# Both attentions of a two-layer decoder trunk rebuilt for four heads at a time

## The chip, the cores and the metric

The kernel runs on one core of one Trainium2 chip. The metric is device time in microseconds (us) of one execution, as the median of several runs. The names of the engines are those of the profile: PE is TensorE's matrix multiplication, PEld its weight load, DVE is VectorE, ACT is ScalarE, POOL is GpSimd and SP is SyncE, which here only issues DMA transfers.

## What is computed

A decoder trunk of two layers on x of shape (1, 256, 1024) in float32. Each layer is an attention and then an MLP with a squared ReLU. Layer 0's attention (MoBA) has 16 heads of 64; its blocks are as long as the sequence, so that each query sees only its own block and the attention is plain causal softmax. Layer 1's attention has 12 heads in three groups of four, with windows and dilations of (128, 1), (512, 4) and (2048, 16); the results of the groups are weighted by their softmax denominators, so that the three groups of one head slot form one softmax. q and k are rotated first in both.

```python
def apply_rotary(t, cos, sin):
    t1, t2 = jnp.split(t, 2, axis=-1)
    return jnp.concatenate([t1 * c - t2 * s, t2 * c + t1 * s], axis=-1)

def sq_relu_mlp(x, w_in, w_out):                       # 1024 -> 4096 -> 1024
    return jnp.square(jax.nn.relu(x @ w_in)) @ w_out

h = x
for i in range(2):
    mix = (moba_attention, dilated_attention)[i](h, w_qkv, w_o, cos, sin)
    h = layer_norm(4 ** 0.25 * h + mix, ln_mix_g[i], ln_mix_b[i])
    h = layer_norm(4 ** 0.25 * h + sq_relu_mlp(h, mlp_w_in[i], mlp_w_out[i]), ln_mlp_g[i], ln_mlp_b[i])
```

## The kernel before

**Precision.** The products use the fp32r type. Each float32 operand is split into a high part (the rounded copy) and a low part (the rest), and a product is three matmuls: high by high, high by low and low by high. `split` (L321) makes the two parts, the high one on ACT (L323) and the low one on DVE (L328). `mm` (L332) issues every matmul but the transposes (L627).

**Weights.** SP loads each weight tile of 128 x 1024 (512 KB) into one of four `raw` buffers; ACT and DVE split it into `whi` and `wlo`, ten buffers of each (`NSLOT`). The kernel uses some 180 such tiles, each once. The layer's input stands transposed in `xs`: 1024 features on the partitions of eight tiles, 256 tokens in the columns, the high part beside the low part, so that 512 columns are both.

**Projections.** q and k come out transposed (features on the partitions). The first four q/k tiles are multiplied while x and the weights arrive (`Stage`). For the other q/k tiles `mm_wstat` (L454) runs 24 matmuls of 256 columns each. For an MLP input tile `mm_wstat_wide` (L467) runs 8 of 512 columns (the high weight with both parts of x at once) and 8 of 256 (the low weight with the high part); the two halves of the PSUM bank are added when it is read. The values and the first MLP chunk have x as the stationary operand (`mm_xstat`, L480), and so have all output projections (`mm_rows`, L506): one weight row of 128 x 1024 takes 12 matmuls of 512 columns, for two halves m of the tokens, two accumulators of 512 columns each and three terms.

**Attention.** Heads go in pairs. `rotate` (L536) turns one q and one k tile: ACT copies each half of the tile to the other half's partitions, DVE multiplies by cosine and sine and adds, then q is split into `qhi` and `qlo`, and k is split twice with a mask (`hm`) that keeps one head's rows, into `khi` and `klo` for both heads side by side. `score` (L588) is three matmuls on all 128 rows, for one half of the queries and both heads' keys: 512 columns, or 256 where a half of the queries needs only a half of the keys. Masking with the row's extreme is on DVE (`mask_min`), the exponential with its sum on ACT (`exps`), the scaling on DVE. For the value product the probabilities are transposed on PE into a `tp` bank and copied to `pt` on ACT (L635); `weigh` (L638) then runs a pair of matmuls, each on 64 of PE's columns, one for each head. A stretch of such column-split matmuls between full ones is called a visit here; before, each has one pair of heads. `attn_out` splits the result into `ahi` and `alo` for the output projection.

**Layer norm.** `ln_half` (L708) adds the residual to the accumulators of one half of the tokens, and normalizes. Where something follows, four transposes (L627) bring 512 features of the half into a `tp` bank, from which ACT and DVE write `xs`. The last MLP has m = 1's second accumulator cut into two of 256 columns, one of them in a `tp` bank (`new_acc`, L757), for all of its 32 weight rows.

**PSUM.** There are four `acc` and four `tp` banks. q/k and output accumulators use `acc`; scores, transposes, value products and MLP input tiles use `tp`.

**What sets the order.** No engine's order is written by hand. The program describes its operations in the order of the strings `ORDER0` and `ORDER1` (a step `qk` projects and rotates a pair, `v` projects values, `s` is a pair's scores and softmax, `o` its transposes and value product; `x`, `g` and `b` are loads), with an estimated cost for each. `Plan.order` (L139) then works out a due time for every operation, back from PE's order, and fills each engine's queue by earliest start and earliest due time, with the buffers of every tag as a limit (a tag in `LOOSE` may be taken out of turn if a spare buffer is left). `TAIL` says how many of the last weight rows are done accumulator by accumulator and not row by row.

Of the kernel before, what the change touches and what calls it, by code (L numbers as in the profile page):

```python
# [40 lines left out]
STAGE_HOME = (("raw", 4),) * 4 + (("g", 1), ("b", 1)) + (("tok", 2),) * 2  # L41
# [49 lines left out]
class Plan:  # L91
# [47 lines left out]
    def order(self):  # L139
        clock = {e: BEGIN[e] for e in ("PE", "SP")}  # L140
        bus = 0.0
        for o in self.ops:
            t = max([clock.get(o.eng, 0.0)] + [p.end + latency(p, o) for p in o.preds])
            o.end = t + o.cost
            if o.eng in clock:
                clock[o.eng] = o.end
            if o.xfer:
                bus = o.end = landed(t, bus, o.xfer)
            o.due = t - o.ahead if o.eng == "PE" else None
        t = clock["PE"]  # L150
# [20 lines left out]
        def start_of(o):  # L171
# [7 lines left out]
            for tag, bs in need.items():  # L179
                q = self.queue[tag]  # L180
                spare = 0
                if {id(b) for b in q[: len(bs)]} != {id(b) for b in bs}:
                    if tag not in LOOSE:
                        return None
                    spare = 1
# [65 lines left out]
LOOSE = ("tp",)  # L251

# [4 lines left out]
    "bst mx sm mv rstd ta raw whi wlo g b xs0 xs1 tok m1 ahi alo ropet khi klo v sc1 sc0 pt0 pt1 qhi qlo ident"  # L257
# [5 lines left out]
def tile_trunk(  # L263
# [17 lines left out]
    hmask: bass.AP,  # L281
# [55 lines left out]
    def load_w(src, n=1024):  # L337
        w = W()
        w.raw = mk([P, 1024], F32, "raw", 4)
# [82 lines left out]
    idle = mk([P, 512], F32, "ta", 4)  # L422
# [11 lines left out]
    hm = const(hmask, [P, 2], "hm")  # L434
# [19 lines left out]
    def mm_wstat(ps, w):  # L454
        def go_hi(kt):
            for part in range(2):
                mm(ps.t[:, :S], w.hi.t[:, kt * P : (kt + 1) * P], xs[kt // 4].t[:, kt % 4, part, :], kt + part == 0, False)

        def go_lo(kt):
            mm(ps.t[:, :S], w.lo.t[:, kt * P : (kt + 1) * P], xs[kt // 4].t[:, kt % 4, 0, :], False, kt == KT - 1)  # L460

        for kt in range(KT):
            op("PE", 0.24, lambda kt=kt: go_hi(kt), [(w.hi, 0)] + xk(kt, (0, 1)), [ps])
        for kt in range(KT):
            op("PE", 0.12, lambda kt=kt: go_lo(kt), [(w.lo, 0)] + xk(kt, (0, 1)), [ps])

    def mm_wstat_wide(ps, w):  # L467
        def go_hi(kt):
            both = xs[kt // 4].t[:, kt % 4, :, :].rearrange("p h s -> p (h s)")
            mm(ps.t, w.hi.t[:, kt * P : (kt + 1) * P], both, kt == 0, False)  # L470

        def go_lo(kt):
            mm(ps.t[:, S:], w.lo.t[:, kt * P : (kt + 1) * P], xs[kt // 4].t[:, kt % 4, 0, :], False, kt == KT - 1)

        for kt in range(KT):
            op("PE", 0.229, lambda kt=kt: go_hi(kt), [(w.hi, 0)] + xk(kt, (0, 1)), [ps])
        for kt in range(KT):
            op("PE", 0.12, lambda kt=kt: go_lo(kt), [(w.lo, 0)] + xk(kt, (0, 1)), [ps])
# [27 lines left out]
    def mm_rows(pieces, item, m):  # L506
        (ahi, alo, j), w, pos, total = item
        first, last = pos == 0, pos == total - 1
# [27 lines left out]
    def rotate(ps, ropet):  # L536

        a = mk([P, 512], F32, "ta", 4)
        b = mk([P, 512], F32, "ta", 4)

        def cols(t, i):
            return t.t[:, i * S : (i + 1) * S]

        for i in range(2):
            for h in range(2):
                op(
                    "ACT", act(S),
                    lambda i=i, h=h: nc.scalar.activation(  # L548
                        cols(b, i)[64 * h : 64 * h + 64], ps[i].t[64 - 64 * h : 128 - 64 * h, :S], AF.Copy
                    ),  # L550
                    [ps[i]], [(b, (i, h))],
                )
        for i in range(2):
            tt(S, lambda i=i: cols(a, i), lambda i=i: ps[i].t[:, :S], lambda: ropet.t[:, 0, :], ALU.mult,
               [ps[i], ropet], [(a, i)])
        for i in range(2):
            k = [(b, (i, h)) for h in range(2)]
            tt(S, lambda i=i: cols(b, i), lambda i=i: cols(b, i), lambda: ropet.t[:, 1, :], ALU.mult, k + [ropet], k)
            tt(S, lambda i=i: cols(a, i), lambda i=i: cols(a, i), lambda i=i: cols(b, i), ALU.add, k + [(a, i)], [(a, i)],
               ADD_ENG)  # L560
        q = mk([P, S], F32R, "qhi", 2), mk([P, S], F32R, "qlo", 2)
        split(S, lambda: a.t[:, :S], lambda: q[0].t, lambda: q[1].t, [(a, 0)], [q[0]], [q[1]], sbuf=True)
        hi, lo = mk([P, 2, S], F32R, "khi", 2), mk([P, 2, S], F32R, "klo", 2)
        for h in range(2):
            op(
                "ACT", act(S, 1, True),
                lambda h=h: nc.scalar.activation(hi.t[:, h, :], a.t[:, S:], AF.Copy, scale=hm.t[:, h : h + 1]),  # L567
                [(a, 1), hm], [(hi, h)],
            )
# [558 lines left out]
```

## Time and profile before

| | |
|---|---|
| median of 3 runs | 574.01 us (573.71 to 574.57) |
| span of the profiled execution | 572.5 us |
| DVE, ACT and PE busy, 296 to 380 us (layer 1's attention) | 71.68, 54.88 and 82.93 of 84 us |
| DVE and ACT busy, 135 to 157 us (first MLP) | 18.16 and 15.24 of 22 us |
| read from HBM | 104.01 MB, 184 GB/s over the span |

The first stretch up to 10 us fills the pipeline; layer 0's attention follows, to about 110 us, then the first MLP, layer 1's attention and from about 390 us the second MLP. Busy times are shares of the engine's own time; PE's records overlap each other, so its busy time doesn't say how densely it is filled. A weight load (PEld) lies beside the matmul ahead of it.

### The profile page before, as it was taken

Reading aid. Unit: us, or ns where it says so; the run is one execution under the profiler, and the core shown is the slowest. Engines: PE = TensorE matmul, PEld = TensorE weight load, DVE = VectorE, ACT = ScalarE, POOL = GpSimd, SP = SyncE. Lnnn points to the kernel's source line nnn. Section 1 sums busy time; section 2 is a strip of 40 time slices with the busy share of each in tenths; the row PEclk is TensorE's granted clock in tenths of the full one; section 3 lists DMA queues with packets and bytes.
Section 4 is the critical chain, followed back from the end, with each engine's and each line's share of the span. In section 5 each row is a group of like instructions: output and inputs, shape, how many; then the busy total and the mean of one; then the engine's idle time right before and its main releaser. Section 6 shows DMA issues by size and latency. Waiting matters only on the chain.

```text
span 572.5 us, 8665 instructions
## 1 busy us (share of the span) xinstructions
PE 561.6 (98%) x3234; PEld 487.1 (85%) x3234; DVE 422.6 (74%) x771; ACT 320.6 (56%) x557; POOL 8.4 (1%) x13
## 2 busy tenths in 40 slices
PE   8999999999999999999999999999999999999994
PEld 7898888788888888888888997888888888888884
DVE  5899788898775675675678798987975756756644
ACT  6988688547654454455534678745754544544400
POOL 0000000010000000000000000000000000000000
PEclk9999999999999999999999999999999999999999
DMA  8657652627885765555625434444888655655001
GB/s 319 228 185 259 230 174 76 224 76 261 295 295 195 222 210 189 185 189 181 192 76 184 172 111 148 149 145 148 266 286 262 212 186 186 189 183 181 37 1 73
DMA packets 30281, 105.61 MB, mean 184 GB/s; under 512 B 3488, under 2 KB 4256, under 8 KB 30240
## 3 DMA queue, kind: packets, MB, share of 16 engines
q1 hardware_dynamic: 30240, 105.07, 55.4%
q8 instruction: 25, 0.41, 0.3%
q14 instruction: 16, 0.13, 0.1%
HBM read 104.01 MB, written 1.05 MB: 184 GB/s over the span
## 4 chain that ended last, share of the span: by engine, by line
PE 91%; ACT 3%; DMA 2%; DVE 2%; SPq 0%; issue 0%; DVEq 0%
PE acc L332 51%; PE tp L332 37%; PE tp L627 2%; DMA raw<-in_wv_dram 1%; DMA g<-in_xw_dram 1%; DVE wlo L328 1%; ACT whi L323 1%; ACT ta L548 1%; ACT sc L613 1%; DVE tok L533 0%; SPq L319 0%; ACT khi L567 0%; DVE ta L526 0%; DVE sc L603 0%; ACT ta L791 0%
## 5 line engine op out<-in xcount | busy, mean ns | idle before, releaser
L328 DVE TENSOR_TENSOR wlo<-raw,whi 128x1024 fp32r<-128x1024 f32 (+2 forms) x185 | 221.9, 1205 | 86.5 <-ACT whi L323 85.8
L323 ACT ACTIVATE whi<-raw 128x1024 fp32r<-128x1024 f32 (+2 forms) x184 | 191.6, 1048 | 137.2 <-PE tp L332 59.2
L332 PE MATMUL acc<-whi,ahi 128*128 128x512 f32 (+1 forms) x312 | 119.3, 382 | 0.0
L332 PE MATMUL acc<-wlo,ahi 128*128 128x512 f32 (+1 forms) x312 | 117.3, 380 | 0.0
L332 PE MATMUL tp<-xs,whi 128*128 128x512 f32 x448 | 112.0, 392 | 0.0
L332 PE MATMUL acc<-whi,alo 128*128 128x512 f32 (+1 forms) x312 | 100.7, 379 | 0.0
L332 PEld LDWEIGHTS tp<-xs,whi 128*128 128x128 f32 x448 | 81.1, 189 | 14.9
L332 PEld LDWEIGHTS acc<-whi,ahi 128*128 128x128 f32 x312 | 58.7, 188 | 11.0 <-issue 0.5
L332 PEld LDWEIGHTS acc<-wlo,ahi 128*128 128x128 f32 x312 | 58.7, 188 | 10.5
L332 PE MATMUL acc<-xs,whi 128*128 128x256 f32 x448 | 65.8, 289 | 0.3 <-ACT xs L323 0.3
L332 PEld LDWEIGHTS acc<-whi,alo 128*128 128x128 f32 x312 | 57.1, 188 | 10.4
L332 PEld LDWEIGHTS tp<-xs,wlo 128*128 128x128 f32 x448 | 61.1, 190 | 4.3
L332 PE MATMUL tp<-xs,wlo 128*128 128x256 f32 x448 | 62.8, 283 | 0.0
L332 PEld LDWEIGHTS acc<-xs,whi 128*128 128x128 f32 x448 | 59.3, 194 | 3.2 <-issue 1.7
L323 ACT ACTIVATE ahi<-ta 128x256 fp32r<-128x256 f32 x56 | 22.9, 409 | 27.0 <-DVE ta L533 26.7
L332 PE MATMUL acc<-xs,wlo 128*128 128x256 f32 x224 | 36.7, 286 | 0.0
L332 PEld LDWEIGHTS acc<-xs,wlo 128*128 128x128 f32 x224 | 31.4, 194 | 0.3 <-issue 0.3
L526 DVE TENSOR_TENSOR ta<-tp,ta 128x256 f32<-128x256 f32 x56 | 23.5, 419 | 10.0 <-ACT ta L781 10.0
L781 ACT ACTIVATE ta<-tp 128x256 f32<-128x256 f32 x56 | 21.1, 377 | 15.3 <-PE tp L332 15.2
L332 PE MATMUL acc<-whi,xs 128*128 128x512 f32 (+1 forms) x112 | 28.4, 363 | 0.0
L328 DVE TENSOR_TENSOR alo<-ta,ahi 128x256 fp32r<-128x256 f32 x56 | 23.4, 420 | 5.9 <-ACT ahi L323 5.9
L548 ACT ACTIVATE ta<-acc 64x256 f32<-64x256 f32 x56 | 21.2, 379 | 10.7 <-DVE ta L526 9.8
(85 smaller groups left out, 537.9 us busy)
## 6 DMA issues: line engine op xcount, KB each, us to landing
raw<-in_win_dram SPq DMA_DIRECT2D x64, 512.0 KB, 4.2
raw<-in_wout_dram SPq DMA_DIRECT2D x64, 512.0 KB, 4.3
raw<-in_wqk_dram SPq DMA_DIRECT2D x24, 512.0 KB, 4.4
raw<-in_wo_dram SPq DMA_DIRECT2D x14, 512.0 KB, 3.5
raw<-in_wv_dram SPq DMA_DIRECT2D x8, 512.0 KB, 5.7
g<-in_lng_dram SPq DMA_DIRECT2D x4, 512.0 KB, 5.3
b<-in_lnb_dram SPq DMA_DIRECT2D x4, 512.0 KB, 6.7
raw<-in_wv1a_dram SPq DMA_DIRECT2D x4, 512.0 KB, 3.3
```

Source lines behind the costliest of these rows:

```text
L323: op("ACT", act(n, sbuf=sbuf), lambda: nc.scalar.activation(hi(), src(), AF.Copy), r, whi)
L328: lambda: nc.vector.tensor_tensor(lo(), src(), f32(hi()), op=ALU.subtract), list(r) + list(whi), wlo,
L332: nc.tensor.matmul(out_ap, lhsT, rhs, start=start, stop=stop)
L526: op("DVE", dve(n) + extra, lambda: nc.vector.tensor_tensor(out_ap(), a(), b(), op=alu), r, w)
L548: lambda i=i, h=h: nc.scalar.activation(cols(b, i)[64 * h : 64 * h + 64], ps[i].t[64 - 64 * h : 128 - 64 * h, :S], AF.Copy),
L613: lambda: nc.scalar.activation(e(), e(), AF.Exp, bias=bias(), scale=-1.0, accum_out=total()), r, w,
L627: nc.tensor.transpose(ps.t[:, c : c + P], src(), ident.t)
L781: op("ACT", act(S), lambda: nc.scalar.activation(u(), ps.t[:, S:], AF.Copy), [ps], uk)
```

## The change

**Order.** `ORDER0` and `ORDER1` go by quads of four heads: four quads in layer 0, three in layer 1 (where a quad has two of the three groups' pairs, `quads`), and in layer 1 one `o` step for each unit of three pairs. The planner's due times also regard the operations that wait for a PSUM bank to come free; `SPARE` is 2 and not 1; `NSLOT` is 9 and not 10; `raw` has 5 buffers and not 4; `ta` has three of 1024 columns and not four of 512.

**q and k.** `mm_wide` takes the place of `mm_wstat` and `mm_wstat_wide`, for q/k and MLP tiles alike: four tiles at a time, the first four k tiles of each with the high weight, then the last four of each, then the low weights. The host lays the four tiles of a quad out as q first halves, k first halves, q second halves, k second halves of four heads, 32 features of a head below each other. So the rotation needs no exchange of partitions and the scores no head mask; `hm` and its DMA go.

**Scores.** Each matmul has 32 rows, one head's half: two halves, three terms, 256 columns or 128, and each head writes a `tp` bank of its own. Four heads stand next to each other in the order.

**Value products.** A visit has two pairs (layer 0) or three (layer 1); `pt` has four buffers of 512.

**MLP.** Chunks of four tiles by `mm_wide`. In the last MLP `new_acc` cuts nothing; the cut of the last accumulator begins at the last seven weight rows, whose `tp` piece is added by DVE to the residual apart.

```diff
-TAIL = (5, 5, 6, 8)
-NSLOT = 10
+TAIL = (5, 5, 6, 7)
+NSLOT = 9
+ORDER0 = "qk-0 v-0 qk-1 s-0 o-0 qk-2 s-1 x-0 x-1 o-1 qk-3 s-2 g-0 v-1 s-3 o-2 b-0 o-3"
...
-ORDER1 = "v-01 qk-0 qk-1 s-0 qk-2 s-1 qk-3 s-2 gb-0 qk-4 s-3 o-0 o-1 o-2 qk-5 s-4 s-5 v-10 v-11 o-3 o-4 o-5"
+ORDER1 = "qk-0 qk-1 s-0 qk-2 s-1 gb-0 s-2 v-01 v-10 v-11 o-0 o-1"
+AHEAD1 = (14.0, 6.0)
...
+    def mm_wide(pss, ws):
...
+        def go_hi(ps, w, k0):
+            for kt in range(k0, k0 + 4):
+                both = xs[kt // 4].t[:, kt % 4, :, :].rearrange("p h s -> p (h s)")
+                mm(ps.t, w.hi.t[:, kt * P : (kt + 1) * P], both, kt == 0, False)
+
+        def go_lo(ps, w):
+            for kt in range(KT):
+                mm(ps.t[:, S:], w.lo.t[:, kt * P : (kt + 1) * P], xs[kt // 4].t[:, kt % 4, 0, :], False, kt == KT - 1)
...
+        for k0 in (0, 4):
+            for j, (ps, w) in enumerate(zip(pss, ws)):
+                op("PE", 4 * 0.2268, lambda ps=ps, w=w, k0=k0: go_hi(ps, w, k0), [(w.hi, 0)] + x(k0, k0 + 4),
+                   [ps, (mark, (k0, j))])
+        for ps, w in zip(pss, ws):
+            op("PE", 0.965, lambda ps=ps, w=w: go_lo(ps, w), [(w.lo, 0), mark] + x(0, KT), [ps])
...
+    def rotate(pss, ropet, wide=True):
+
+        u, a, b = [mk([P, 4, S], F32, "ta", 3) for _ in range(3)]
+        for i, ps in enumerate(pss):
+            op("ACT", act(S), lambda i=i, ps=ps: nc.scalar.activation(u.t[:, i, :], ps.t[:, S:] if wide else ps.t[:, :S], AF.Copy),
+               [ps], [(u, i)])
+            if wide:
+                tt(S, lambda i=i: u.t[:, i, :], lambda ps=ps: ps.t[:, :S], lambda i=i: u.t[:, i, :], ALU.add,
+                   [ps, (u, i)], [(u, i)])
...
+            for dst, k in ((a, 0), (b, 1)):
+                tt(512, lambda c=c, dst=dst: dst.t[:, c, :], lambda c=c: u.t[:, c, :],
+                   lambda k=k: ropet.t[:, k : k + 1, :].broadcast_to([P, 2, S]), ALU.mult,
+                   [(u, i) for i in keys] + [ropet], [(dst, h)])
...
+            tt(512, lambda c=c: a.t[:, c, :], lambda c=c: a.t[:, c, :], lambda d=d: b.t[:, d, :], ALU.add if h else ALU.subtract,
+               [(a, h), (b, 1 - h)], [(a, h)])
+            split(512, lambda c=c: a.t[:, c, :], lambda h=h: hi.t[:, h, :, :], lambda h=h: lo.t[:, h, :, :],
+                  [(a, h)], [(hi, h)], [(lo, h)], sbuf=True)
...
+    def score(pss, qk, blocks):
...
+            for i in range(max(len(bl) for bl in blocks)):
+                for h in range(2):
+                    for t, (a, b) in enumerate(((hi, hi), (hi, lo), (lo, hi))):
+                        for n, bl in enumerate(blocks):
+                            if i >= len(bl):
+                                continue
+                            qc, kc, off = bl[i]
+                            r = slice(32 * n, 32 * n + 32)
+                            mm(pss[n].t[:, off : off + kc.stop - kc.start], a.t[r, h, 0, qc], b.t[r, h, 1, kc],
+                               h + t == 0, h + t == 3)
...
+            for p in range(2):
+                weigh(o, p * S, v[0], vc + p * P, pts[p], 0, S, 0, True, False)
+                weigh(o, p * S, v[1], vc + p * P, pts[2], p * S, P, P, False, True)
...
+    def pv_dilated(e, v, vcs, ahi, alo, ahead):
...
+            for kb in range(2):
+                weigh(o, 0, v[0][kb], vcs[0], full[kb], 0, S, 0, kb == 0, kb == 1)
+            for m in range(2):
+                weigh(o, S, v[1][m], vcs[1], diag[0], m * S, P, m * P, True, True)
+                weigh(o2, 0, v[2][m], vcs[2], diag[1], m * S, P, m * P, True, True)
...
-    def new_acc(last=False):
-        acc = [[(psum("acc"), n * 512, 512) for n in range(2)] for _ in range(2)]
-        if last:
-            acc[1] = [acc[1][0], (acc[1][1][0], 512, 256), (psum("tp"), 768, 256)]
-        return acc
+    def new_acc():
+        return [[(psum("acc"), n * 512, 512) for n in range(2)] for _ in range(2)]
...
+            if last and m == 1:
+                acc[1] = [acc[1][0], (acc[1][1][0], 512, S), (psum("tp"), 768, S)]
...
+        quads = (((0, 0), (0, 1)), ((0, 2), (1, 0)), ((1, 1), (1, 2)))
```

The change moves instructions on PE in three places. The first is layer 0's first scores, on PE. `tp` are PSUM banks; `acc_338` (before) and `acc_406` (after) are q/k accumulators, the rows on them the last of a projection. `mm` is L332 before and L345 after. Before:

```order
L332 MATMUL acc_338<-wlo_305,xs_2_75 128x512 x2
L332 MATMUL tp_396<-khi_81,qhi_88 128x512
L332 MATMUL tp_396<-klo_82,qhi_88 128x512
L332 MATMUL tp_396<-khi_81,qlo_89 128x512
L332 MATMUL tp_402<-khi_81,qhi_88 128x256
L332 MATMUL tp_402<-klo_82,qhi_88 128x256
L332 MATMUL tp_402<-khi_81,qlo_89 128x256
```

And after, where the first eight of a quad's 48 score matmuls are shown:

```order
L345 MATMUL acc_406<-xs_2_75,wlo_366 128x256 x4
L345 MATMUL tp_488<-rhi_80 128x256
L345 MATMUL tp_490<-rhi_80 128x256
L345 MATMUL tp_492<-rhi_80 128x256
L345 MATMUL tp_494<-rhi_80 128x256
L345 MATMUL tp_488<-rlo_81,rhi_80 128x256
L345 MATMUL tp_490<-rlo_81,rhi_80 128x256
L345 MATMUL tp_492<-rlo_81,rhi_80 128x256
L345 MATMUL tp_494<-rlo_81,rhi_80 128x256
```

Six matmuls for a pair, into two banks, became groups of four that go round four banks, one for each head.

The second place is the head of layer 1 on PE: the last transposes of the layer norm's second half (`tok` into `tp`), behind them the value projection of the first half (`acc` from `xs` and a weight's high part). Before:

```order
L627 MATMUL tp_3139<-ident_90,tok_719 128x128 x4
L627 MATMUL tp_3145<-ident_90,tok_719 128x128 x4
L332 MATMUL acc_3103<-whi_2967,xs_2_75 128x512 x2
L332 MATMUL acc_3103<-whi_2985,xs_2_75 128x512 x2
L332 MATMUL acc_3161<-whi_2900,xs_1_74 128x512
L332 MATMUL acc_3161<-wlo_2922,xs_1_74 128x512
L332 MATMUL acc_3161<-whi_2900,xs_1_74 128x512
```

After:

```order
L631 MATMUL tp_3055<-ident_86,tok_373 128x128 x4
L631 MATMUL tp_3061<-ident_86,tok_373 128x128 x4
L345 MATMUL acc_3019<-whi_2895,xs_2_75 128x512 x2
L345 MATMUL acc_3019<-whi_2916,xs_2_75 128x512 x2
L345 MATMUL acc_3074<-xs_1_74,whi_2984 128x512 x4
L345 MATMUL acc_3083<-xs_1_74,whi_2997 128x512 x4
L345 MATMUL acc_3092<-xs_1_74,whi_3014 128x512 x4
```

The value projection of the second half (`acc_3161`), which stood next, moved far behind; the first wide q/k matmuls stand there now.

The third place is the value products of layer 1's first unit on PE, with `pt` (transposed probabilities) and `v`; `acc_3659` is a q/k tile. Before, a visit for each of the unit's three pairs, here the first two:

```order
L332 MATMUL acc_3659<-xs_1_74,whi_3389 128x256 x2
L332 MATMUL tp_3694<-pt_692_3674,v_3164 64x256 x2
L332 MATMUL tp_3694<-pt_694_3683,v_3212 64x256 x2
L332 MATMUL acc_3659<-xs_2_75,whi_3389 128x256 x2
L332 MATMUL tp_3714<-pt_697_3697,v_3164 64x128 x2
L332 MATMUL tp_3714<-pt_697_3697,v_3212 64x128 x2
```

After, one visit for the three pairs, with `acc_3688` a value projection:

```order
L345 MATMUL acc_3688<-whi_3401,xs_2_75 128x256 x2
L345 MATMUL tp_3759<-pt_3726,v_3079 64x256 x2
L345 MATMUL tp_3759<-pt_3732,v_3677 64x256 x2
L345 MATMUL tp_3759<-pt_3740,v_3079 64x128 x2
L345 MATMUL tp_3766<-pt_3746,v_3079 64x128 x2
L345 MATMUL tp_3759<-pt_3740,v_3677 64x128 x2
L345 MATMUL tp_3766<-pt_3746,v_3677 64x128 x2
L345 MATMUL acc_3688<-whi_3401,xs_2_75 128x256 x2
L631 MATMUL tp_3788<-ident_86,e_3555 128x128
```

Three visits of one pair became one visit of three, and it moved from among q/k tiles to the end of the last value projection; the second unit's transposes follow it.

More of the change, by code (lines that the diff above doesn't have):

```diff
@@ L251 @@
 LOOSE = ("tp",)
+SPARE = 2
 BANKS = ("tp", "acc")
 LAYOUT = (
-    "bst mx sm mv rstd ta raw whi wlo g b xs0 xs1 tok m1 ahi alo ropet khi klo v sc1 sc0 pt0 pt1 qhi qlo ident"
+    "bst mx sm mv rstd ta raw whi wlo g b xs0 xs1 tok m1 ahi alo rhi rlo v e pt ropet ident"
 ).split()
@@ L338, in load_w @@
         w = W()
-        w.raw = mk([P, 1024], F32, "raw", 4)
+        w.raw = mk([P, 1024], F32, "raw", 5)
         w.hi = mk([P, 1024], F32R, "whi", NSLOT)
@@ L504, in mm_xstat, with mm_rows @@
                 )
-    def mm_rows(pieces, item, m):
+    def mm_rows(pieces, item, m, opens=False):
         (ahi, alo, j), w, pos, total = item
-        first, last = pos == 0, pos == total - 1
+        first, last = pos == 0 or opens, pos == total - 1
         t = slice(m * P, (m + 1) * P)
@@ L534, in stt @@
         )
[L536 to L563, printed above, removed]
-        for h in range(2):
[L565 to L569, printed above, removed]
-            stt(
-                S, 1, lambda h=h: lo.t[:, h, :], lambda: a.t[:, S:], lambda h=h: hm.t[:, h : h + 1],
-                lambda h=h: f32(hi.t[:, h, :]), ALU.mult, ALU.subtract, [(a, 1), hm, (hi, h)], [(lo, h)],
-            )
-        return q, (hi, lo)
@@ L583, in tile_trunk @@
+    def proj_qk(ws):
+        pss = [psum("acc") for _ in ws]
+        mm_wide(pss, ws)
+        return pss
     first_ps = [psum("acc") for _ in range(NFIRST)]
@@ new lines, in weigh, with attn_out @@
+    def weigh(o, o0, v, vc, pt, p0, n, c0, start, stop):
+        for h in range(2):
+            c = slice(vc + 64 * h, vc + 64 * h + 64)
+            mm(o.t[64 * h : 64 * h + 64, o0 + c0 : o0 + c0 + n], v.t[:, c],
+               pt.t[:, p0 + h * n : p0 + (h + 1) * n], start, stop)
+    def attn_out(o, o0, n, ahi, alo, j, src):
+        keys = [(j + i, m) for i in range(n) for m in range(2)]
+        if src:
+            get = lambda: o.t[:, o0 : o0 + S].rearrange("p (c b a) -> p a b c", a=4, b=4)
+            put = lambda t: t.t[:, j, :].rearrange("p (a b c) -> p a b c", a=4, b=4)
+        else:
+            get = lambda: o.t[:, o0 : o0 + n * S]
+            put = lambda t: t.t[:, j : j + n, :].rearrange("p j s -> p (j s)")
+        split(n * S, get, lambda: put(ahi), lambda: put(alo), [o], [(ahi, k) for k in keys], [(alo, k) for k in keys])
@@ L822, in rest @@
             self.half(1)
-            acc = new_acc(self.last)
+            acc = new_acc()
             nkt = DFF // P
@@ new lines, in layer1 @@
+                for u, gi in quads[n]:
+                    if u not in units:
+                        units[u] = (
+                            [[mk([P, 512], F32, "e", 8) for _ in range(2)] for m in range(2)],
+                            mk([P, NG, 4], F32, "mx3", 2),
+                            mk([P, 8], F32, "sm", 4),
+                        )
+                    for h in range(2):
+                        pss.append(psum("tp"))
+                        if gi == 0:
+                            blocks.append([(halves[m], slice(0, S), m * S) for m in range(2)])
+                        else:
+                            blocks.append([(halves[m], halves[m], m * P) for m in range(2)])
@@ L1037, in _layout, with quads @@
     d = {"x": x[perm]}
-    pair = np.concatenate([np.arange(32), 64 + np.arange(32), 32 + np.arange(32), 96 + np.arange(32)])
+    def quads(w, heads):
+        parts = []
+        for four in heads:
+            for half in range(2):
+                for s in range(2):
+                    for h in four:
+                        parts.append(w[:, s, h, 32 * half : 32 * half + 32])
+        return np.concatenate(parts, axis=1)
     def col_tiles(w):
```

356 lines of the change are left out of this document (156 added, 200 removed).

## The prediction

> **What bounds the kernel now.** I start with the page's first two parts and its chain of waits.
>
> ```profile
> span 572.5 us, 8665 instructions
> PE 561.6 (98%) x3234; PEld 487.1 (85%) x3234; DVE 422.6 (74%) x771; ACT 320.6 (56%) x557; POOL 8.4 (1%) x13
> PEclk9999999999999999999999999999999999999999
> PE 91%; ACT 3%; DMA 2%; DVE 2%; SPq 0%; issue 0%; DVEq 0%
> ```
>
> PE is busy for 98% of the span at the full granted clock, and 91% of the chain that ends last runs through it. The profiled execution spans 572.5 us; the median of the three timed runs is 574.0, so 1.5 us lie around the span, and I leave them as they are. What the list of waits says of PE matters next.
>
> ```profile
> PE tp L332 <- DVE warm L416: 1.2, 1, 1.2
> PE tp L627 <- ACT pt L635: 1.1, 1, 1.1
> PE tp L332 <- ACT xs L323: 0.6, 2, 0.3
> ```
>
> These are the three longest of PE's own waits, 2.9 us together, the first of them before any work. So the kernel is bound by PE's work, and a change is worth what it takes from PE, minus what it makes PE wait. A busy PE is still not a PE at its peak, so I take no mean durations from the groups (they overlap) but the pace at which pieces of the chain follow each other:
>
> ```profile
> 144.35 10.91 PE acc L332 x48
> 155.26 11.15 PE tp L332 x64
> ...
> 324.10 5.75 PE acc L332 x48
> 329.85 0.72 PE tp L332 x6
> ...
> 409.01 2.07 PE acc L332 x10
> 411.80 2.07 PE acc L332 x10
> ```
>
> The first piece is four weight rows of the first MLP's output, 48 matmuls of 512 columns: 10.91 / 48 = 0.227 us each. The third is two q/k weight tiles, 48 matmuls of 256 columns: 0.120 each. The fourth is six score matmuls of 256 columns, again 0.120. The second is four MLP input tiles, 32 wide and 32 of 256 columns: 11.15. The last two are the same kind of weight row as the first, in the second MLP: 2.79 from one to the next, where the first MLP takes 10.91 / 4 = 2.73.
>
> **The change, term by term.**
>
> *Wide q/k.* Each of 24 q/k tiles outside the first four now runs as an MLP input tile does, 8 wide and 8 narrow matmuls, not 24 narrow ones. Four tiles took 2 x 5.75 = 11.50 and should take 11.15: 0.35 for each of six quads, **-2.1**. The MLP's regrouping into chunks of four keeps the number and the shapes of its matmuls: 0.
>
> *Second MLP's output.* 25 of 32 weight rows no longer cut the last accumulator into two halves of 256: 25 x (2.79 - 2.73) = **-1.5**. The last seven rows keep the cut. The tail after the last matmul should keep its length:
>
> ```profile
> 564.01 0.42 DVE L533 SCALAR_TENSOR_TENSOR tok<-tok,acc 128x256 f32<-128x256 f32 x1 [1.75 <-PE acc L332]
> 565.08 0.42 DVE L533 SCALAR_TENSOR_TENSOR tok<-tok,tp 128x256 f32<-128x256 f32 x1 [0.19 <-PE tp L332]
> ```
>
> The first of these becomes 512 wide, but 12 narrow matmuls (1.4 us) now follow its accumulator's last one, before the bank that ends the work; it ends earlier than that.
>
> *Scores.* Before, there are 36 matmuls of 512 columns and 48 of 256:
>
> ```profile
> L332 PE MATMUL tp<-khi,qhi 128*128 128x512 f32 x12 | 4.8, 403 | 0.0
> ...
> L332 PE MATMUL tp<-khi,qhi 128*128 128x256 f32 x16 | 4.6, 287 | 0.0
> ```
>
> Three such groups each make 36 x 0.227 + 48 x 0.120 = 13.9 us. After, there are 336 matmuls on quarters of PE's rows, in 84 slots of four (36 of 256 columns, 48 of 128). The trace of before has none on quarters of rows. Bounds: one after another, at 0.120 and at the 0.109 that a 128-column transpose takes (below), they cost 4 x (36 x 0.120 + 48 x 0.109) = 38.2; four beside each other cost a quarter, 9.6. The nearest rows are the value products, which use halves of PE's columns:
>
> ```profile
> 366.37 1.91 PE L627 MATMUL tp<-ident,sc 128*128 128x128 f32 x16
> 368.21 1.52 PE L332 MATMUL tp<-pt,v 128*64 128x256 f32 x16
> ...
> 370.92 0.40 PE L332 MATMUL acc<-whi,alo 128*128 128x512 f32 x1
> 371.25 0.66 PE L332 MATMUL tp<-pt,v 128*64 128x128 f32 x8
> 371.84 0.50 PE L332 MATMUL acc<-whi,ahi 128*128 128x512 f32 x1
> 372.17 0.39 PE L332 MATMUL acc<-wlo,ahi 128*128 128x512 f32 x1
> 372.40 0.40 PE L332 MATMUL acc<-whi,alo 128*128 128x512 f32 x1
> ```
>
> Sixteen transposes fill 368.21 - 366.37 = 1.84, with some 0.1 for the step to the next kind: 0.109 each. Eight value records of the same width fill 371.84 - 371.25 = 0.59; one after another they would need 0.87. So two halves do run beside each other, 4 slots x 0.109 = 0.44 and the rest is for changing over. I take the same for quarters: 9.6, **-4.3**.
>
> The Trainium skill (page "TensorE: Matmul & The Clock Gate", section "Measured speedup vs the span model") reports for four row tiles of 32 rows and 512 columns a gain of 3.07, not 4. By it the scores would cost an estimated 38.2 / 3.07 = 12.4, and the time would be about 568; the rows on column halves agree that tiles overlap, and no row here shows tiles of rows.
>
> *Changing over.* From 370.92 to 372.40 pass 1.48 us; three wide matmuls and four slots account for 3 x 0.227 + 0.44 = 1.12. A visit to the split array so costs 0.36. Before, the order on PE has 15 such visits, all for values; after, 6 for values and 7 for scores: 2 x 0.36 = **-0.7**. A visit of scores loads 128 columns, not 64, before it starts; I add half a slot, 0.05, for each: **+0.35** (bounds 0 and 7 x 0.36 = 2.5 for a second changeover's worth). The value products and transposes themselves stay: same counts, same shapes.
>
> *Waits that go and come.* The 1.1 us on `pt` fell on layer 1's first unit, whose transposes and value visits stood among q/k tiles; it goes: **-1.1**. What is late next? First, the head of layer 1:
>
> ```profile
> 303.73 1.04 PE L627 MATMUL tp<-ident,tok 128*128 128x128 f32 x8
> 304.54 1.42 PE L332 MATMUL acc<-whi,xs 128*128 128x512 f32 x5
> ```
>
> ```profile
> 303.80 0.68 DVE L328 TENSOR_TENSOR xs<-tp,xs 128x512 fp32r<-128x512 f32 x1
> 304.40 1.21 DVE L328 TENSOR_TENSOR wlo<-raw,whi 128x1024 fp32r<-128x1024 f32 x1
> 305.54 1.28 DVE L328 TENSOR_TENSOR xs<-tp,xs 128x512 fp32r<-128x512 f32 x2
> ```
>
> Before, after the transposes PE had 0.9 us of value projection and then the other half's, which opens with xs's high parts. After, the 0.9 us are followed at once by the wide q/k matmuls, which read high and low parts together. DVE no longer puts a weight split between, so the low part comes about 0.6 earlier, ends near 305.7 and is usable near 305.95; PE is there at 303.73 + 0.87 + 0.91 = 305.5: **+0.45** (0 to 1.2, a weight split of DVE in between after all). Behind the waiting matmul stand two quads of q/k on PE; nobody else is late.
>
> Second, the end of layer 1, where scores, transposes and outputs share four tp banks:
>
> ```profile
> L323 ACT ACTIVATE whi<-raw 128x1024 fp32r<-128x1024 f32 x180 | 189.2, 1058 | 134.9 <-PE tp L332 59.2 <-PE acc L332 54.9 <-DMA raw<-in_win_dram 8.6
> ...
> L635 ACT ACTIVATE pt<-tp 128x512 f32<-128x512 f32 x16 | 9.1, 591 | 2.2 <-PE tp L627 2.1
> L613 ACT ACTIVATE sc<-sc,mx 128x256 f32<-128x256 f32 x16 | 8.0, 503 | 2.6 <-DVE mx L603 2.5
> ...
> L613 ACT ACTIVATE sc<-sc,mx 128x128 f32<-128x128 f32 x16 | 6.2, 391 | 0.0
> ...
> L323 ACT ACTIVATE ahi<-tp 128x512 fp32r<-128x512 f32 x4 | 2.4, 599 | 1.8 <-PE tp L627 1.7
> ```
>
> The second unit's third transpose group needs the bank that holds the first unit's output, free after a split on ACT (0.60) and one on DVE (0.69), with hand-offs some 1.6 us behind the value visit; PE reaches it after a changeover, two matmuls and two transpose groups, 0.24 + 0.24 + 0.87 = 1.35. The fourth group and its copy follow, so I take **+0.4** (0 to 1.6); behind it on PE stand the output's first rows. In layer 0 the first transposes stand 20 to 24 wide matmuls, 4.5 to 5.4 us, behind a quad's scores. The first two heads' exponentials need 2 x 0.50 + 2 x 0.39 = 1.8 on ACT, and a mask before and scalings behind them about 1; the other two heads as much again, and their transposes stand later: 0.
>
> *Work off PE.* Per quad the rotation on DVE was 14 x 0.42 + 4 x 0.48 = 7.8 us and becomes 4 x 0.42 + 8 x 0.69 = 7.2; on ACT 14 instructions become 6. The durations are these rows':
>
> ```profile
> L533 DVE SCALAR_TENSOR_TENSOR klo<-ta,hm,khi 128x256 fp32r<-128x256 f32 x28 | 12.5, 480 | 1.1 <-ACT khi L567 0.7
> ...
> L526 DVE TENSOR_TENSOR ta<-ta,ropet 128x256 f32<-128x256 f32 x28 | 11.7, 421 | 2.4 <-ACT ta L548 2.1
> ...
> L328 DVE TENSOR_TENSOR alo<-tp,ahi 128x512 fp32r<-128x512 f32 x4 | 2.7, 686 | 2.3 <-ACT ahi L323 2.3
> ```
>
> PE hides it, before and after; were that cover gone, DVE would bind layer 0, where it stands at 84.75 of 95 us:
>
> ```profile
> 10.00:105.00 95.00, 94.78 (x646) 83.03 (x645) 84.75 (x220) 78.59 (x183) 0.00 (x0) 1.00 0.58 202
> ```
>
> The columns after the length are PE, weight loads, DVE and ACT. One weight slot less and one raw buffer more cost nothing in the MLPs: a tile comes every 2.8 us, and splitting one takes 1.06 on ACT and 1.21 on DVE. The DMAs are the same but for the small head mask, which goes.
>
> **The sum:** -2.1 - 1.5 - 4.3 - 0.7 + 0.35 - 1.1 + 0.45 + 0.4 = -8.5. The span comes to 564.0, the time to 574.0 - 8.5 = **565.5**.
>
> **The rivals.**
>
> *Quarters limited by issue.* A slot of four is eight instructions, four loads and four matmuls. The densest that the trace shows is the visit at 371.25: 16 in 0.44 us, 27 ns each. At that pace a slot costs 0.218, the scores 84 x 0.218 = 18.3 and the time is 565.5 + 8.7 = 574.2, no change. For it: nothing here shows a faster pace. Against it: nothing shows that this pace was issue and not the two matmuls' 0.109. Between the two paces the time lies anywhere from 567.5 to 574.2.
>
> *Quarters run one after another,* so that the change doesn't do what it says: 38.2 us of scores, and 565.5 + 28.6 = **594**, slower. It decides from the point where the scores cost 13.9 and the other terms' 4.2 together, 18.1 us or 0.215 a slot: if fewer than about two of four overlap, the change loses. Against it speak the column halves.
>
> *Hand-offs take the place of the matmuls.* The copies of four heads now stand one behind the other on ACT, and the value visit waits for the last; if each of the six visits finds a weight split (1.06) ahead of its copy and waits so long, that is +6.4, 571.9. For it: the 1.1 us on `pt` is such a wait. Against it: in 95 us of layer 0 before, PE waited hardly at all with DVE at 89%.
>
> **How the numbers follow.** Forecast 0.62, within 563.5 to 567.5 (bounds of the changeover, of the two waits, and a share of overlap lost). Issue-limited 0.15, spread from 567.5 to 574.2. Hand-offs 0.12, up to 571.9. One after another 0.10. Something cheaper than I think, 0.01. The range 563.5 to 571.9 leaves out the last third of the issue-limited case, the quarters one after another and a little of the forecast, together under 0.2. About 0.2%, 1.1 us, is what a measurement of this kernel can tell from no change. Faster by more: 0.62 + 0.01, 0.11 of the issue-limited case and 0.10 of the hand-offs, 0.84; within it 0.03 and 0.02 of these two, 0.05; slower 0.10, and 0.01 of the issue-limited case, 0.11.
>
> **What would show it.** In the chain, 11.15 us for a q/k quad and 10.91 for four weight rows of the second MLP. A score visit of a layer-0 quad near 1.4 us for 48 matmuls, whose four quarters start within a few ns; 2.6 would be the issue limit, 5.4 one after another. PE's waits by line: under 1 us on xs and on pt or tp banks each, else the hand-offs. PE busy share still 98%. The prediction is wrong if DVE or ACT takes more than a few per cent of the chain in either attention, or if the score visits are over 2 us.

## The result, and the profile after

| | before | after |
|---|---|---|
| median of 4 runs | 574.29 us (573.71 to 574.73) | 563.66 us (563.01 to 563.92) |
| span of the profiled execution | 572.5 us | 561.9 us |

The ratio is 0.9816 (95% interval 0.9802 to 0.9829): 10.6 us faster. The forecast was 565.5, within 563.5 to 571.9; the result lies 0.2 us above the lower end. The page of the changed kernel, with its busy times and its chain of waits by engine:

```profile
span 561.9 us, 8502 instructions
PE 551.7 (98%) x3219; PEld 471.3 (84%) x3219; DVE 408.6 (73%) x729; ACT 298.2 (53%) x495; POOL 8.4 (1%) x13
PE 90%; DVE 6%; ACT 1%; DMA 1%; issue 1%; SPq 0%; DVEq 0%; ACTq 0%
```

PE is as full as before, with 10 us less to do. Its waits, all that the list has (engine and line, what was waited for, total us, times, longest):

```profile
PE tp L345 <- DVE warm L429: 1.2, 1, 1.2
PE tp L345 <- ACT xs L336: 0.6, 2, 0.3
PE tp L631 <- DVE alo L341: 0.4, 1, 0.4
PE acc L345 <- DVE xs L341: 0.4, 1, 0.4
PE acc L345 <- ACT xs L336: 0.2, 1, 0.2
```

The 1.1 us on `pt` is gone; `alo` is the end of layer 1, and the two lines on `acc` belong to the start, at 6.8 and 9.3 us. There is no wait in layer 0's attention, and none on the list at the head of layer 1. There the timeline shows a small delay:

```profile
299.12 1.20 PE L345 MATMUL acc<-whi,xs 128*128 128x512 f32 x4
300.32 0.96 PE L345 MATMUL acc<-xs,whi 128*128 128x512 f32 x3
```

The last of the four starts at 299.92, and the first wide q/k matmul 0.40 behind it where 0.227 is the pace: it is late by 0.2. Now the pace, in pieces of the chain (start, length, what). The first row holds a value projection of 24 wide matmuls and the first q/k quad, the others are output rows and input tiles of the two MLPs:

```profile
23.57 16.52 PE acc L345 x88
...
139.27 10.91 PE acc L345 x48
150.17 11.09 PE tp L345 x64
...
400.53 10.91 PE acc L345 x48
411.43 11.09 PE tp L345 x64
```

Four input tiles take 11.09, not 11.15, and the second MLP's output rows now take 10.91 for four, as the first's. A visit of scores in layer 0, from the timeline (start, us from the first start to the last end, shape as rows*columns of PE):

```profile
39.33 0.76 PE L345 MATMUL acc<-xs,wlo 128*128 128x256 f32 x5
40.02 0.39 PE L345 MATMUL tp<-rhi 32*128 32x256 f32 x4
40.24 0.29 PE L345 MATMUL tp<-rlo,rhi 32*128 32x256 f32 x4
40.36 0.29 PE L345 MATMUL tp<-rhi,rlo 32*128 32x256 f32 x4
...
40.83 0.24 PE L345 MATMUL tp<-rhi 32*128 32x128 f32 x4
40.89 0.29 PE L345 MATMUL tp<-rlo,rhi 32*128 32x128 f32 x4
41.00 0.29 PE L345 MATMUL tp<-rhi,rlo 32*128 32x128 f32 x4
41.11 0.29 PE L345 MATMUL tp<-rhi 32*128 32x128 f32 x4
...
41.56 0.72 PE L345 MATMUL acc<-xs,whi 128*128 128x512 f32 x2
```

Each row is one slot of four quarters. Slots follow each other after 0.12 us with 256 columns and after 0.11 with 128, which is what one such matmul takes on all rows: the four run beside each other. The visit ends 1.54 us after its first start, the changing over at its end included.

Where the time went, stage by stage, from the same places in both traces. The stretch before is from the first matmul of 512 columns (17.73 before, 17.94 after) to the layer norm's first transposes, the others go on from there, to the last transposes of the first MLP's layer norm, to the second MLP's first four output rows and to PE's last matmul. The forecast's terms are split by stage:

| stage | before | after | difference | forecast |
|---|---|---|---|---|
| layer 0's attention | 17.73 to 116.98 | 17.94 to 111.92 | -5.3 | -4.4 |
| first MLP | to 303.89 | to 298.47 | -0.4 | 0 |
| layer 1's attention and the second MLP's head | to 409.01 | to 400.53 | -3.1 | -2.6 |
| second MLP | to 564.77 | to 554.27 | -2.0 | -1.5 |

Every stage gave somewhat more than was forecast.

### The profile page after: what moved, and what is told of

Read it like the earlier page. It is cut to its first block, busy times and chain, and to the rows that moved or that the text cites. A ratio compares the mean times of both kernels' runs of the same rounds, so it can differ in the third digit from the quotient of the medians.

```text
span 561.9 us, 8502 instructions
## 1 busy us (share of the span) xinstructions
PE 551.7 (98%) x3219; PEld 471.3 (84%) x3219; DVE 408.6 (73%) x729; ACT 298.2 (53%) x495; POOL 8.4 (1%) x13
## 4 chain that ended last, share of the span: by engine, by line
PE 90%; DVE 6%; ACT 1%; DMA 1%; issue 1%; SPq 0%; DVEq 0%; ACTq 0%
PE acc L345 52%; PE tp L345 36%; PE tp L631 2%; DVE ta L539 2%; DVE wlo L341 2%; DVE e L607 1%; DMA raw<-in_xw_dram 1%; DVE e L624 1%; ACT whi L336 0%; DVE rlo L341 0%; DVE tok L546 0%; SPq L332 0%; ACT ta L798 0%; ACT xs L336 0%; ACT e L617 0%
## 5 line engine op out<-in xcount | busy, mean ns | idle before, releaser
L336 ACT ACTIVATE whi<-raw 128x1024 fp32r<-128x1024 f32 (+2 forms) x184 | 187.4, 1046 | 143.9 <-PE acc L345 70.3
L345 PE MATMUL acc<-whi,ahi 128*128 128x512 f32 (+1 forms) x312 | 121.7, 390 | 0.0
L345 PE MATMUL acc<-wlo,ahi 128*128 128x512 f32 (+1 forms) x312 | 120.9, 387 | 0.0
L345 PE MATMUL tp<-xs,whi 128*128 128x512 f32 x448 | 104.5, 390 | 0.0
L345 PE MATMUL acc<-whi,alo 128*128 128x512 f32 (+1 forms) x312 | 103.0, 387 | 0.0
L345 PEld LDWEIGHTS tp<-xs,whi 128*128 128x128 f32 x448 | 83.9, 188 | 17.5
L345 PEld LDWEIGHTS acc<-whi,alo 128*128 128x128 f32 x312 | 58.6, 188 | 12.1
L345 PEld LDWEIGHTS acc<-whi,ahi 128*128 128x128 f32 x312 | 58.7, 188 | 11.5 <-issue 0.3
L345 PEld LDWEIGHTS acc<-wlo,ahi 128*128 128x128 f32 x312 | 58.7, 188 | 11.2
L345 PE MATMUL acc<-xs,whi 128*128 128x512 f32 (+1 forms) x256 | 59.6, 373 | 0.6 <-DVE xs L341 0.4
L345 PEld LDWEIGHTS tp<-xs,wlo 128*128 128x128 f32 x448 | 55.6, 192 | 1.1
L345 PE MATMUL tp<-xs,wlo 128*128 128x256 f32 x448 | 55.9, 283 | 0.0
L345 PEld LDWEIGHTS acc<-xs,whi 128*128 128x128 f32 x256 | 46.3, 193 | 9.3 <-DVE xs L341 1.4
L345 PE MATMUL acc<-xs,wlo 128*128 128x256 f32 x224 | 33.5, 285 | 0.0
L345 PEld LDWEIGHTS acc<-xs,wlo 128*128 128x128 f32 x224 | 30.4, 193 | 0.8 <-issue 0.3
L345 PE MATMUL acc<-whi,xs 128*128 128x512 f32 (+1 forms) x112 | 28.4, 365 | 0.0
L345 PE MATMUL tp<-whi,xs 128*128 128x512 f32 x80 | 24.6, 395 | 0.6 <-ACT xs L336 0.6
L546 DVE SCALAR_TENSOR_TENSOR tok<-tok,acc 128x512 f32<-128x512 f32 x16 | 11.0, 686 | 16.7 <-PE acc L345 16.6
```

The source lines that it names most:

```text
L336: op("ACT", act(n, sbuf=sbuf), lambda: nc.scalar.activation(hi(), src(), AF.Copy), r, whi)
L345: nc.tensor.matmul(out_ap, lhsT, rhs, start=start, stop=stop)
L546: lambda: nc.vector.scalar_tensor_tensor(dst(), a(), s(), b(), op0=o0, op1=o1), r, w,
```

## The experiments

All start from the changed kernel. Two numbers are given for each: the time against the changed kernel (the median less 0.9816 of the median that the kernel before had on the same chip, 574.67 to 574.82), and the difference of PE's **steady stretch** in the profiled execution, from the first matmul of 512 columns to the last matmul: 536.33 us in the changed kernel, 547.04 before. The first has a 95% interval of some 0.8 us either way (1.7 for the first run), so the small effects are read from the second, which is one execution of each. The stretch leaves out the start, which differs from run to run: the first 512-column matmul began between 17.13 and 18.83 us in these eleven traces, as x and the first weights arrived.

| run | median us | time, us | stretch, us | theory |
|---|---|---|---|---|
| heads one by one | 598.01 | +33.9 | +34.5 | +29 |
| two quarters | 570.18 | +6.1 | +6.6 | +9.7 |
| narrow q/k | 566.05 | +2.0 | +2.4 | +2.5 |
| tile by tile | 565.20 | +1.1 | +1.4 | +1.3 |
| halved rows | 564.90 | +0.7 | +1.6 | +1.4 |
| v first | 566.77 | +2.5 | +3.4 | -0.3 |
| alternating | 567.40 | +3.2 | +4.3 | -4.2, 0 or +8.6 |
| planner undone | 564.21 | 0.0 | +1.0 | 0 to +1 |
| visits apart | 564.83 | +0.7 | +1.3 | +1.4 |

**Scores, one head after the other.** Only the loops' order differs.

```diff
-            for i in range(max(len(bl) for bl in blocks)):
-                for h in range(2):
+            for four in ((0,), (1,), (2,), (3,)):
+                for i in range(2):
+                    for h in range(2):
...
-                        for n, bl in enumerate(blocks):
+                            for n in four:
```

> The changed kernel (563.7 us) with the scores' loops turned: each head's twelve matmuls stand together, the four heads one behind the other. Theory (four quarters of rows run beside each other only because neighbours in the order use different rows): each of the 336 matmuls gets a slot of its own, 0.118 us at 256 columns and 0.110 at 128 as in the changed kernel's trace; 84 slots at a mean of 0.115 become 336, so +29 us, about 593. Rival (the engine overlaps quarters however they are ordered, or the price is set by how fast instructions are issued): 563.7, no change.

It took 598.0. So the overlap is a matter of order: neighbours must use different rows. But the sum is made otherwise than I expected. From the first start of a visit to the first matmul behind it (1.54 for the one above), the seven visits take 33.4 us and not 10.9: 22.5 more, not 29, since the next head's first three matmuls start beside the last three of the head before. The other 12 us are in the matmuls behind the visits. First two rows of its timeline, then three windows around the end of that visit, with PE's granted clock in the third column from the right (1.00 is full speed):

```profile
44.57 0.34 PE L345 MATMUL tp<-rhi,rlo 32*128 32x128 f32 x1
44.84 2.93 PE L345 MATMUL acc<-xs,whi 128*128 128x512 f32 x6
```

```profile
30.00:40.00 10.00, 10.00 (x60) 8.91 (x59) 6.95 (x10) 4.73 (x8) 0.00 (x0) 1.00 0.96 358
44.70:48.00 3.30, 3.30 (x10) 2.51 (x10) 3.02 (x13) 3.09 (x11) 0.00 (x0) 0.50 0.00 0
48.10:56.00 7.90, 7.90 (x46) 6.73 (x44) 4.60 (x11) 3.77 (x7) 0.00 (x0) 1.00 0.00 0
```

Six wide matmuls take 2.93 us, where in the changed kernel two take 0.72 and each further one 0.227: after a visit with one quarter at work at a time, the clock is at half for over 3 us though PE never paused.

**Scores, two heads at a time.** As above, with `((0, 1), (2, 3))`.

> The changed kernel with the scores done for two heads at a time, so two quarters of rows beside each other and not four. Theory (a slot has a length of its own, 0.118 or 0.110 us, however many quarters are in it): 168 slots and not 84, +84 x 0.115 = +9.7 us, about 573.4. Rival (a slot of four is limited by issue, 8 instructions in 0.115, 14 ns each): two quarters need half the time, so 563.7, no change.

Two pieces of its chain, a score visit and the q/k matmuls behind it:

```profile
40.98 2.52 PE tp L345 x43
43.51 5.68 PE acc L345 x24
```

The visit takes 2.52 us where four quarters take 1.54. With half the instructions in a slot the slot stays as long (0.11 to 0.12 from start to start), so that it isn't issue that limits it; the rival falls. The +9.7 that I expected isn't reached either: the second pair's first slots already run beside the last slots of the first pair, on other rows. The clock stays at 1.00 here, and the 24 matmuls behind take 5.68 as in the changed kernel.

**Narrow q/k tiles.**

```diff
+    def mm_narrow(pss, ws):
...
+                for part in range(2):
+                    mm(ps.t[:, :S], w.hi.t[:, kt * P : (kt + 1) * P], xs[kt // 4].t[:, kt % 4, part, :], kt + part == 0, False)
...
+                mm(ps.t[:, :S], w.lo.t[:, kt * P : (kt + 1) * P], xs[kt // 4].t[:, kt % 4, 0, :], False, kt == KT - 1)
...
-        mm_wide(pss, ws)
+        mm_narrow(pss, ws)
...
-            return rotate(proj_qk([load_w(wqk0[4 * p + i - NFIRST]) for i in range(4)]), ropes[0])
+            return rotate(proj_qk([load_w(wqk0[4 * p + i - NFIRST]) for i in range(4)]), ropes[0], False)
```

The MLP tiles keep `mm_wide`. The `False` leaves out DVE's addition of a bank's two halves; layer 1's call changes alike.

> The changed kernel with the 24 q/k tiles done by 24 matmuls of 256 columns each, as before the change, still four tiles at a time; all else as changed. Theory (PE alone sets what the wide tiles are worth): six quads at 11.50 and not 11.09 us, +2.5, about 566.1. Rival (DVE is late in layer 1, and loses 24 additions of 0.42 us here, so that PE's waits of 0.6 and 0.2 us there go): +1.6, about 565.3.

The stretch is 2.4 longer. The chain's piece that holds a value projection and a quad:

```profile
23.76 16.95 PE acc L345 x120
```

16.95 against 16.52 above: 0.43 for a quad, and 6 x 0.43 = 2.6. PE's wait at the end of layer 1 doesn't shrink, though DVE has 24 additions less to do: it grows from 0.4 to 0.6, while the 0.2 at the head of the layer goes. The wide tiles are worth what PE saves; the waits about cancel.

**Wide projections tile by tile.**

```diff
-        for k0 in (0, 4):
-            for j, (ps, w) in enumerate(zip(pss, ws)):
-                op("PE", 4 * 0.2268, lambda ps=ps, w=w, k0=k0: go_hi(ps, w, k0), [(w.hi, 0)] + x(k0, k0 + 4),
-                   [ps, (mark, (k0, j))])
         for ps, w in zip(pss, ws):
-            op("PE", 0.965, lambda ps=ps, w=w: go_lo(ps, w), [(w.lo, 0), mark] + x(0, KT), [ps])
+            for k0 in (0, 4):
+                op("PE", 4 * 0.2268, lambda ps=ps, w=w, k0=k0: go_hi(ps, w, k0), [(w.hi, 0)] + x(k0, k0 + 4), [ps, mark])
+            op("PE", 0.965, lambda ps=ps, w=w: go_lo(ps, w), [(w.lo, 0)] + x(0, KT), [ps, mark])
```

> The changed kernel with the wide projections done tile by tile, 8 matmuls of 512 columns and then 8 of 256 for each, as the MLP had it before the change; 32 wide and 32 narrow ones for four tiles otherwise. Theory (each return from narrow to wide matmuls costs about 0.02 us, on the five wide ones behind it): three more returns in each of 20 chunks, 20 x 3 x 0.021 = +1.3, about 564.9, with 11.15 us for a chunk again. Rival (the 11.15 of before came from banks or from work of other engines): 563.7, and 11.09.

Four tiles take 11.15 us again:

```profile
151.09 11.15 PE tp L345 x64
```

That the stretch grows by 1.4, close to the 1.3 expected, is partly luck: in layer 0 a wait of 0.8 on a weight's low part came in, and the wait of 0.4 at the end of layer 1 went. In the two MLPs, where the waits are the same, 14 chunks cost 0.7. So the change's regrouping of the MLP input tiles, which I had at nothing, gives some 0.06 for each of 14 chunks, 0.7 to 0.8 us. In the traces of both kernels the first five wide matmuls behind a run of narrow ones start 0.233, 0.236, 0.229, 0.233 and 0.231 after each other, and then 0.227; the first narrow one behind wide ones takes 0.113 and the further ones 0.120. A return so costs 0.028 less 0.006.

**The last accumulator in halves,** for 24 of the second MLP's weight rows.

```diff
+            parts = [(acc, c0, 0, n) for acc, c0, n in pieces]
+            if halves2:
+                acc, c0, n = pieces[1]
+                parts[1:] = [(acc, c0, 0, S), (acc, c0 + S, S, S)]
...
+            for acc, c0, o, n in parts:
+                mm(acc.t[:, o : o + n], a, w.hi.t[:, c0 : c0 + n], first, False)
...
```

> The changed kernel with 24 of the last MLP's 25 full weight rows doing the last accumulator of m = 1 in two halves of 256 columns, six narrow matmuls instead of three wide ones, as before the change but in one bank. Theory (a return from narrow to wide and the narrow ones' own pace cost 2.79 - 2.73 a row): 24 x 0.06 = +1.4, about 565.1. Rival (the 0.06 of before came from the second bank, a tp bank): 563.7.

Four rows take 11.15 and not 10.91, 0.06 each, and 24 x 0.06 = 1.4 of the stretch's 1.6:

```profile
421.91 11.15 PE acc L345 x60
```

The cost of before lay in the narrow matmuls and not in the second bank.

**Layer 1's second value projection first.**

```diff
-ORDER1 = "qk-0 qk-1 s-0 qk-2 s-1 gb-0 s-2 v-01 v-10 v-11 o-0 o-1"
+ORDER1 = "v-01 qk-0 qk-1 s-0 qk-2 s-1 gb-0 s-2 v-10 v-11 o-0 o-1"
```

> The changed kernel with layer 1's second value projection ahead of its first q/k quad, as before the change. Theory (the wait of PE on xs at the head of layer 1 is 0.2 to 0.4 us and goes, as work that needs the high parts only stands there): -0.3, about 563.4, and no more, since what is late next is the 0.6 us at the end of the layer. Rival (DVE is the late engine in layer 1, and the projection's 1.8 us of PE work at the head gives it nothing but a later start of q/k): the wait at the end grows to over 1 us, 564.2.

Both expectations were wrong: 2.5 us slower, 3.4 in the stretch. Its waits of PE, the four longest but the start's:

```profile
PE tp L631 <- DVE e L624: 0.8, 2, 0.6
PE tp L345 <- ACT xs L336: 0.6, 2, 0.3
PE tp L631 <- ACT pt L641: 0.3, 1, 0.3
PE tp L631 <- DVE mx L607: 0.3, 1, 0.3
```

The delay at the head of the layer is gone, as expected. At its end PE now waits for the last softmax (`e`, `mx`) and for `pt`, some 1.5 us in all: the projection, 24 matmuls of 512 columns or 5.4 us (not the 1.8 of my rival), was what lay between the last scores and their transposes. The waits are less than half of the 3.4. Behind the first of them the granted clock falls:

```profile
349.30:351.70 2.40, 1.49 (x8) 0.85 (x9) 2.40 (x14) 0.89 (x4) 0.00 (x0) 1.00 0.00 0
351.80:355.10 3.30, 3.30 (x18) 2.59 (x18) 3.14 (x12) 3.30 (x9) 0.00 (x0) 0.50 0.00 0
```

In the second window PE is busy throughout, but its transposes start 0.213 after each other and not 0.109: 3.3 us at half pace lose about 1.6. The change's place for the projection hides more than it costs.

**Wide and narrow alternating.**

```diff
                 mm(ps.t, w.hi.t[:, kt * P : (kt + 1) * P], both, kt == 0, False)
-
-        def go_lo(ps, w):
-            for kt in range(KT):
                 mm(ps.t[:, S:], w.lo.t[:, kt * P : (kt + 1) * P], xs[kt // 4].t[:, kt % 4, 0, :], False, kt == KT - 1)
...
-        for ps, w in zip(pss, ws):
-            op("PE", 0.965, lambda ps=ps, w=w: go_lo(ps, w), [(w.lo, 0), mark] + x(0, KT), [ps])
```

> The changed kernel with wide and narrow matmuls of the same k tile alternating in every wide projection (80 tiles of 8 and 8). Theory A (narrow ones in a row take 0.120 and not 0.113 because their weight loads are not hidden; behind a wide one they are): 640 x 0.0065 = -4.2 us, about 559.5, an 11.09 us chunk becomes 10.88. Theory B (each return from narrow to wide costs as the five wide ones behind a narrow run show it, 0.007 on the first alone): the gain is given back, 563.7. Theory C (a whole 0.02 for each return): 640 x (0.02 - 0.0065) = +8.6, 572.3.

None of the three. Four tiles take 11.29:

```profile
149.94 11.29 PE tp L345 x64
```

That is 0.20 more than in long runs, and 20 x 0.20 = 4.0 of the stretch's 4.3. A pair takes 0.353 on average, where long runs give 0.227 + 0.120 = 0.347: what a narrow matmul gains behind a wide one, the wide ones lose again. Long runs of one width are the best of the three orders tried.

**The planner's share undone.**

```diff
-            for q in frees.get(o, ()):
-                d = q.due - o.cost - latency(o, q)
-                o.due = d if o.due is None else min(o.due, d)
...
-SPARE = 2
+SPARE = 1
...
-        w.raw = mk([P, 1024], F32, "raw", 5)
+        w.raw = mk([P, 1024], F32, "raw", 4)
```

> The changed kernel with the planner's share of the change undone: due times without the operations that wait for a PSUM bank, one spare bank and not two, four raw buffers and not five. The instructions and their shapes stay, only the order on the engines is another. Theory (PE's work is what the change saved, the order only has to keep PE fed): within 1 us, 563.7 to 564.7. Rival (the order of bank use is what keeps the hand-offs of four heads covered): waits of the size that was forecast for them, up to +6.4, 570.

No difference in time (0.9815 of before; interval 0.9801 to 0.9830), 1.0 us in the stretch, of which half is a longer delay on xs at the head of layer 1 (0.7 and not 0.2). The new due times are not what makes the change work.

**Layer 0's value visits apart.**

```diff
-        op("PE", 0.2 + 2 * (0.432 + 0.22), go, [v[0], v[1]] + pts, [o])
...
+        op("PE", 0.2 + 0.432 + 0.22, lambda: go(0, pts[0]), [v[0], v[1]] + pts, [(o, 0), mark])
+        late_pt = turned([blk(h, c) for h in (2, 3) for c in (S, 0)], e[2:4] + [mark])
+        op("PE", 0.2 + 0.432 + 0.22, lambda: go(1, late_pt), [v[0], v[1], late_pt, pts[1]], [(o, 1)])
```

> The changed kernel with layer 0's four joint value visits taken apart: the second pair's transposes wait for the first pair's value products, so that eight visits of one pair stand there again, the same matmuls in them. Theory (a visit to the split array costs 0.36 us in changing over, whatever is in it): +4 x 0.36 = +1.4, about 565.1. Rival (hand-offs: each second pair's copy on ACT now stands between its transposes and its products with little PE work in between, 0.6 for the copy and up to 1.06 for a weight split ahead of it): +1.4 and waits of 4 x 0.6 to 1.6, 567.5 to 571.5.

The stretch grows by 1.3: four visits more, 0.33 each. Two of them, with the transposes and weight rows between:

```profile
50.66 0.80 PE tp L345 x8
51.47 0.59 PE tp L631 x4
52.05 1.91 PE acc L345 x16
53.96 0.80 PE tp L345 x8
```

Each copy finds 1.4 to 1.9 us of PE work to hide behind, and no wait of PE is added. The hand-offs weren't critical even when the cover was as thin as this.

## Why the prediction was right

The kernel was bound by PE's work, and the change was worth what it took from PE: three stages moved the way of their sums, and the first MLP, forecast at nothing, gained 0.4. The sign and the range held, but the range only just, and with luck: the result is 1.8 us below the forecast and 0.2 above the lower end, and one of the four timed runs, 563.01, lies below it. With the score visits' extra and both new waits at their lower bound of 0, the sum comes to 564.3 only. What lies beyond it is mostly one term put at nothing and one cost taken too low, that of the scores before. Point by point:

- *Wide q/k* (-2.1): six quads at 11.09 and not 11.50, -2.5. Undone, it costs 2.4. The size was 0.06 a quad too small, for the reason of the next point.
- *MLP regrouping* (0): wrong. "Keeps the number and the shapes of its matmuls" is true, but their order counts too: 14 x 0.06 = -0.8, of which the run tile by tile gives back 0.7 in the two MLPs. This is the step of the prediction that failed.
- *Second MLP's rows* (-1.5): four rows took (431.33 - 409.01) - 11.15 = 11.17 before and take 10.91, 25 rows -1.6. Undone for 24 rows, 1.4 to 1.6. The tail keeps its length: 7.7 us from the last matmul's start to the end before, 7.6 after.
- *Scores* (from 13.9 to 9.6 and, with 0.36 and 0.05 for each of 7 visits, 12.5): the seven visits take 12.3 with their changing over (10.9 from the first start to the matmul behind, and 0.2 for each around that). Before, the scores took 14.6, 0.7 more than summed up: 0.3 where they stood right behind a value visit, the rest in their own pace, as wide and narrow ones changed places in layer 0. The Trainium skill's 3.07 of 4 (page "TensorE: Matmul & The Clock Gate", section "Measured speedup vs the span model") would have made it an estimated 12.4 without the changing over; here the slots show four of four, and 38.2 / 12.3 = 3.1 only when the changing over is counted in.
- *Changing over* (0.36 a visit): the value visits took 14.2 us in 15 visits and take 10.7 in 6, 0.39 less for each visit that went, and 0.36 without a delay of 0.3 on `pt` at 38.7 us that I hadn't counted. Taken apart again in layer 0, a visit costs 0.33.
- *Waits*: the 1.1 on `pt` went (1.2 from start to start). At the head of layer 1 came 0.2, not 0.45. At its end came 0.4 (0.6 from start to start), as forecast (0.4) and where: the third group of transposes waits for the bank of the first unit's output. What hides the rest there, the value projection, I didn't name; without it the layer takes 3.4 us more, part of it waits and about 1.6 a fallen clock.

The rivals: quarters limited by issue would have shown 0.218 a slot, there are 0.110 to 0.118; eight instructions pass in 0.110, 14 ns each, so that the 27 ns which I read from the value visits was the matmuls' own pace. Quarters one after another exist, if the order makes them so, and are dearer than reckoned, by the clock behind them. Hand-offs stayed hidden.

One of the signs I gave was bad. DVE has 6% of the chain, which I had said would mean that the prediction is wrong. The chain's rows at the end of layer 1:

```profile
354.87 0.68 DVE alo L341
355.55 0.04 issue
355.60 1.09 PE tp L631 x8
```

From that one wait the chain goes back, almost all of it along DVE, which was busy nearly without a gap, to 320 us, and so books some 30 us on DVE. PE waited 0.4 us there. What an engine has of the chain is no measure of what is lost to it; the list of waits, with the steps from start to start, is a better one.

The parts measured in the traces, -2.5 - 0.8 - 1.6 - 5.7 (scores and visits, 14.6 + 14.2 - 12.3 - 10.7) - 1.2 + 0.2 + 0.6, make -11.0 for a stretch that is 10.7 shorter; 0.3 stays unassigned. The scores' share and the waits are read from the two traces: no run puts the old scores into the changed kernel, or takes layer 1's value visits apart.

## What to carry to other kernels

Where PE is full, sum PE's instructions by start-to-start pace, and let the order of widths count: long runs of one width are cheaper than short ones, by 0.02 us for each return to the wide one here. Matmuls on few rows pay only when neighbours in the order use different rows; put the four side by side, and gather them in as few visits as PSUM banks allow. Before moving a block of independent PE work to where it hides a small wait, see what it hides where it stands.

## What the runs showed of the hardware that was not expected

- At the end of score visits with one quarter of the rows at work at a time, 4.5 to 5.5 us long, or just behind them, the granted clock fell to 0.50 (44.7 to 48.0 us, 345.0 to 351.8 us and five times more), and the next 7 to 20 matmuls ran at half pace (wide ones started 0.427 after each other and not 0.227), without any pause of PE. The Trainium skill says (page "TensorE: Matmul & The Clock Gate", section "What's actually happening") that the gate halves the clock by how busy PE has been lately; the halved pace agrees, and here PE issued all the time, with a quarter of its rows at work. With two quarters and visits of 2.5 us the clock stayed full; whether rows or length decide was not tried. With layer 1's value projection first it fell once too, behind a visit of four quarters and PE's waits of 0.3 and 0.6; what of these did it, no run shows.
- A slot of four quarters costs 0.118 us at 256 columns and 0.110 at 128, so that half the columns save next to nothing.
- Wide matmuls behind narrow ones are slowed for five in a row (0.233, 0.236, 0.229, 0.233, 0.231 against 0.227), although each narrow one leaves 0.120.
